# Nine up pairs by seven products, two low parts by accumulating DMA, and half-height score tiles in a two-layer hybrid attention block on Trainium2

## The chip, the core and the metric

The kernel runs on one core of one Trainium2 chip. Its metric is the time of one execution in device microseconds (us), the median of several runs; a profiled execution beside them leaves a trace. The engines are called by the profile's names: PE (TensorE, matmuls), PEld (its weight loads), DVE (VectorE), ACT (ScalarE), POOL (GpSimd) and SP (SyncE, which issues most DMAs). A line number such as L579 is a line of the kernel before.

## The reference, cut to what matters

512 tokens of 1024 features go through two layers, all in float32. Layer 0 has differential attention over all earlier tokens, layer 1 windowed attention with sinks; behind each stands a gated feed-forward block of 2816 hidden features.

```python
def swiglu(h, w_gate_up, w_down):
    g, u = jnp.split(h @ w_gate_up, 2, axis=-1)
    return (jax.nn.silu(g) * u) @ w_down
...
    for l in range(DEPTH):
        h = rms_norm(x, attn_norm[l])
        if l < N_A:
            x = x + diff_attention(h, cos, sin, da_w_qkv[l], ...)
        else:
            if l == N_A:
                kw, vw = shared_kv(x, cos, sin, kv_norm, w_kv, k_norm)
            x = x + swa_sink_attention(h, cos, sin, sw_w_q[j], ..., kw, vw)
        x = x + swiglu(rms_norm(x, ffn_norm[l]), w_gate_up[l], w_down[l])
```

In both attentions the scores are products over a head of 64 features. In layer 0 a pair of score matrices (two half heads) belongs to each head; in layer 1 four query heads share one key head, and a block of 128 queries sees its own block of keys and the one before.

## The kernel before, in words

**Split numbers.** A float32 matrix is multiplied as a sum of three products: each operand is split into a high part `hi` (a cast on ACT, L578, L267, L774) and a low part `lo` (source minus high part, a subtraction on DVE, L579, L268, L775), and PE adds hi·hi, hi·lo and lo·hi in PSUM (`mm3`, L288, and the loops at L704 and L790).

**Order.** PE's instructions are in the order in which the program writes them. The other engines' order is set by the scheduler from priorities; `tc.high_priority(offset=...)` moves a few instructions ahead (constants `BOOST`, `EVAC`, `NPRI`, `HOT`, `SW_BOOST`, `SW_EVAC`). SP issues weight loads in its own order and waits there for a free buffer.

**Attention stages.** Layer 0 works on four pairs of heads. For each, a list (`DA_STEPS`, `DA_STEPS3`) gives slots to the steps T (turn queries and keys, `flip`), C (scores, `score`), U (turn the softmax, `turn`), W (weigh values, `weigh`), N and B (norm); between slots `Fill.pull` writes matmuls of the next pair's projections into PE's order (`DA_FILL` us for a slot unit). `score` (L1009) multiplies half heads of 64 features: two matmuls of 64 rows each, one on the upper and one on the lower half of the array, into two banks. Layer 1 has 16 units of work (4 key heads by 4 query blocks); `SW_AT` holds six slots for each: turn the queries (`turn_q`), two scores, two turns of the softmax, weigh. There `q_evac` (L422) builds a tile whose columns hold a head's high part on 64 rows and its low part on the other 64, with a copy of the keys on both halves, so that a full-height matmul gives hi·hi and lo·hi at once; a score for one head is two matmuls (L1331, L1332), and one call of `score` does two heads.

**Feed-forward block.** The hidden features are cut into 11 pairs `q` of 256 gate and 256 up columns, worked in chunks (0, 1), (2, 3, 4), (5, 6, 7), (8, 9, 10): first the up products of each pair of the chunk, then the down products of the chunk. A plain pair (`up`, L627) takes 96 matmuls of 512 columns. A pair in `FAST` (`up7`, L662) uses a scheme of seven products of half blocks in place of eight: 14 products (seven for gate, seven for up) of 12 matmuls with 256 columns, with sums of weight blocks on DVE (L671, L672, L687, L689) and sums of results (L722 to L739). The down part (`down`, L753) uses the scheme for all pairs: seven factors `s`, each with a right side (weights `g`, `make_right`, four sums for each pair) and a left side (`make_left`), 6 matmuls of 512 columns for each factor and pair. `tokens` (L591) makes the summed token blocks once for a layer.

**Preparation ahead.** `Flow` (L463) writes the splits ahead of their use: `AHEAD` says how many uses ahead, rings of `HLB` = 8 buffers (hi, lo) and `AHB` buffers (left parts) bound it. Weight tiles `r` (up) and `g` (down) have three buffers each.

Of the kernel before, what the change touches and what calls it, by code (L numbers as in the profile page):

```python
# [17 lines left out]
P = 128  # L18
# [11 lines left out]
FAST = (2, 3, 5, 6, 8, 9)  # L30
AHEAD = {'w': 4, 'a': 4}
AHB = 5
WRAW = 3
XDB = 0
BOOST = 42
HOT = 1220
EVAC = 17
# [6 lines left out]
NPRI = 759  # L44
DA_FILL = 0.65


def DA_STEPS(T, C, U, W, N, B):
    return [
        (0, T, 0),  # L50
        (5, C, 0, 0),
        (5.4, T, 1),
        (5.78, C, 0, 1),
        (7.16, C, 1, 0),
        (11, C, 1, 1),
        (11.9, T, 2),
        (13.5, U, 0, 1),
        (17.5, U, 0, 0),
        (17.8, C, 2, 0),
        (19, T, 3),  # L60
        (20.59, U, 1, 0),
        (20.84, C, 2, 1),
        (22.01, W, 0, 0),
        (23.1, U, 1, 1),
        (24.5, C, 3, 0),
        (28.5, W, 0, 1),
        (30.5, N, 0),
        (31.9, C, 3, 1),
# [7 lines left out]
        (47.84, N, 1),  # L76
        (58.9, B, 1),
# [37 lines left out]
SW_K = [4, 5, 6, 12]  # L115
SW_AT = [5.2, 7.3, 8.7, 15.1, 16, 17.8, 8.8, 10.9, 12.3, 18.7, 19.6, 21.3, 10.1, 13.3, 14.8, 21.1, 22, 23.7, 14.7, 16.8, 18.3, 24.6, 25.5, 27.73, 16.7, 19.5, 20.9, 27.3, 28.2, 29.9, 21.66, 23.76, 25.16, 31.56, 32.46, 34.96, 26.5, 28.6, 30, 36.4, 37.3, 39, 31.1, 33.2, 34.6, 41, 41.9, 43.6, 37.3, 39.4, 40.8, 45.7, 48.1, 49.8, 39, 41.1, 42.5, 48.24, 49.8, 51.5, 43.1, 45.2, 46.6, 53.13, 53.9, 55.6, 45.6, 47.7, 49.1, 56.3, 56.83, 58.1, 49.9, 52, 53.4, 60.6, 61.36, 61.69, 52.53, 55.4, 56.8, 64, 64.1, 65.09, 57.5, 59.6, 61, 67.86, 68.3, 70.39, 61.5, 63.6, 65, 72.2, 72.3, 74.39]
SW_R = [-0.4, 13.7, 14.24, 39.07, 43.47, 47.06]
SW_F = 37.2
# [18 lines left out]
def tile_yoco_hybrid(  # L137
# [284 lines left out]
    def q_evac(ap, pt):  # L422
        q = ap.tile([P, 512], F32R, name=nm("q"), tag="q", bufs=QB)
        src = pt[:, 0:256].rearrange("p (s q) -> p s q", q=P)
        dst = q.rearrange("p (s j q) -> p s j q", j=2, q=P)
        a, b = slice(0, HD), slice(HD, P)
        with tc.high_priority(offset=pri["evac"]):
            for j, (own, other) in enumerate(((a, b), (b, a))):
                nc.scalar.copy(dst[own, :, j], src[own])
                nc.vector.tensor_tensor(dst[other, :, j], src[own], dst[own, :, j].bitcast(F32), op=ALU.subtract)  # L430
        return q

# [66 lines left out]
    class Ffn:  # L499
# [69 lines left out]
        def load_r(self, q, j):  # L569
            if q < NQ:  # L570
                r = self.rs[q, j] = self.fp.tile([P, 2, 4, 256], F32, name=nm("r"), tag="r", bufs=WRAW)
                for c in range(2):
                    nc.sync.dma_start(out=r[:, c], in_=self.wu[:, 4 * j:4 * j + 4, c * FFN + q * 256:c * FFN + (q + 1) * 256])

        def split(self, src, shape):
            hi = wp.tile(shape, F32R, name=nm("hi"), tag="hi", bufs=HLB)
            lo = wp.tile(shape, F32R, name=nm("lo"), tag="lo", bufs=HLB)
            nc.scalar.copy(hi, src)  # L578
            nc.vector.tensor_tensor(lo, src, hi.bitcast(F32), op=ALU.subtract)  # L579
# [920 lines left out]
```

## Time and profile before

| | us |
|---|---|
| median of three runs | 1151.5 (1151.07 to 1151.97) |
| the profiled execution | 1150.19 |
| its span in the trace | 1148.1 |
| layer 0 attention, 47 to 268 us of the span | 221.0 |
| layer 0 feed-forward, chunks 2 to 4, 341.9 to 615.3 | 273.4 |
| layer 1 attention, 615.3 to 791 | 175.7 |

Times in a profile line are us from the span's start, or durations; "mean ns" is one instruction's. In the timeline a line gives start, duration, engine, line, operation, out<-in, tile sizes and a count, with the engine's idle time ahead of it in brackets. A matmul's duration includes its way through the array, so matmuls that follow each other overlap in the records: the step from one start to the next is the price. The same holds for DVE. In the table of waits a line is: engine, line, and what it waited for, the sum in us, how often, the longest.

### The profile page before, as it was taken

The numbers are of one execution on the slowest core, as the hardware profiler recorded it, in microseconds if no ns is written. First come the engines' busy times: TensorE is split into PE (matmuls) and PEld (weight loads), VectorE is DVE, ScalarE is ACT, GpSimd is POOL, SyncE is SP. The second block draws the span as 40 slices with busy tenths as digits, with TensorE's granted clock in tenths as the row PEclk, the third lists the DMA queues.
The fourth block names the chain that finished last, engine by engine and source line by source line (L and its number), as shares of the span: only waits on it lengthen the run. The fifth ranks groups of instructions, "written<-read, shape, count | busy, mean of one in ns | idle before, by whom it ended". The sixth has DMA issues, their size and how long they took to land.

```text
span 1148.1 us, 18912 instructions
## 1 busy us (share of the span) xinstructions
PE 1123.8 (98%) x6806; PEld 979.7 (85%) x6806; DVE 995.2 (87%) x2368; ACT 659.4 (57%) x1463; POOL 20.4 (2%) x32
## 2 busy tenths in 40 slices
PE   8999999999999999999999999989999999999998
PEld 7878888778889889989988888777989989988986
DVE  5979798979999998898888797988899898898877
ACT  6565756554556455455446579787545545545533
POOL 0100000000000000000300000000000000000000
PEclk9999999999999999999999999999999999999999
DMA  6312122122723323405202221020634405314201
GB/s 194 111 56 69 47 70 65 47 74 79 252 72 114 109 71 124 137 18 167 76 1 82 84 74 56 20 74 11 206 115 147 144 4 171 98 63 148 74 1 74
DMA packets 86591, 103.29 MB, mean 90 GB/s; under 512 B 5161, under 2 KB 68034, under 8 KB 86498
## 3 DMA queue, kind: packets, MB, share of 16 engines
q1 hardware_dynamic: 86064, 100.97, 27.3%
q0 software_dynamic: 384, 1.11, 0.4%
q8 instruction: 53, 0.87, 0.3%
q14 instruction: 40, 0.33, 0.1%
q10 hardware_dynamic: 50, 0.01, 0.0%
HBM read 99.98 MB, written 2.10 MB: 89 GB/s over the span
## 4 chain that ended last, share of the span: by engine, by line
PE 76%; DVE 16%; ACT 4%; DMA 2%; issue 1%; SPq 0%; DVEq 0%; ACTq 0%
PE acc L706 12%; PE acc L289 10%; PE acc L291 10%; PE acc L290 10%; PE tr L791 9%; PE acc L791 8%; PE tr L706 7%; DVE lo L268 2%; PE po L706 1%; DVE s L1024 1%; DVE hss L382 1%; PE po L791 1%; PE po L290 1%; PE tr L1020 1%; DVE xs L460 1%
## 5 line engine op out<-in xcount | busy, mean ns | idle before, releaser
L578 ACT CAST hi<-g 128x512 fp32r<-128x512 f32 x154 | 95.2, 618 | 113.1 <-PE acc L290 104.4
L578 ACT CAST hi<-r 128x512 fp32r<-128x512 f32 x160 | 98.6, 620 | 75.5 <-PE acc L706 44.2
L289 PE MATMUL acc<-hi,hTh 128*128 128x256 f32 (+1 forms) x384 | 137.6, 358 | 2.7 <-ACT hTh L866 0.9
L291 PE MATMUL acc<-hTh,lo 128*128 128x512 f32 (+1 forms) x384 | 136.4, 355 | 0.7 <-DVE lo L579 0.5
L289 PE MATMUL acc<-hTh,hi 128*128 128x512 f32 (+1 forms) x384 | 136.2, 355 | 0.0
L290 PE MATMUL acc<-hTl,hi 128*128 128x512 f32 (+1 forms) x384 | 136.1, 354 | 0.0
L291 PE MATMUL acc<-hi,hTl 128*128 128x256 f32 (+1 forms) x384 | 130.1, 339 | 0.3 <-DVE hTl L296 0.2
L290 PE MATMUL acc<-lo,hTh 128*128 128x256 f32 (+1 forms) x384 | 129.7, 338 | 0.4 <-DVE lo L268 0.4
L579 DVE TENSOR_TENSOR lo<-r,hi 128x512 fp32r<-128x512 f32 x160 | 106.2, 690 | 18.4 <-ACT hi L578 18.0
L579 DVE TENSOR_TENSOR lo<-g,hi 128x512 fp32r<-128x512 f32 x154 | 105.5, 691 | 12.6 <-ACT hi L578 12.2
L774 ACT CAST ah<-lf 128x256 fp32r<-128x256 f32 x154 | 60.5, 404 | 81.2 <-PE acc L791 32.2
L289 PEld LDWEIGHTS acc<-hi,hTh 128*128 128x128 f32 x384 | 72.9, 190 | 13.5 <-issue 3.7
L291 PEld LDWEIGHTS acc<-hTh,lo 128*128 128x128 f32 x384 | 72.5, 189 | 12.0 <-DVE lo L579 1.3
L267 ACT CAST hi<-raw 128x512 fp32r<-128x512 f32 x96 | 57.4, 618 | 43.8 <-PE acc L291 26.8
L290 PEld LDWEIGHTS acc<-hTl,hi 128*128 128x128 f32 x384 | 72.6, 189 | 10.1 <-DVE hTl L296 0.2
L706 PE MATMUL acc<-th,hi 128*128 128x256 f32 x288 | 81.1, 282 | 0.0
L706 PE MATMUL acc<-tl,hi 128*128 128x256 f32 x288 | 81.1, 282 | 0.0
L706 PE MATMUL acc<-th,lo 128*128 128x256 f32 x288 | 81.0, 281 | 0.0
L289 PEld LDWEIGHTS acc<-hTh,hi 128*128 128x128 f32 x384 | 72.6, 189 | 9.7
L291 PEld LDWEIGHTS acc<-hi,hTl 128*128 128x128 f32 x384 | 72.7, 189 | 9.3 <-DVE hTl L867 0.7
L290 PEld LDWEIGHTS acc<-lo,hTh 128*128 128x128 f32 x384 | 73.1, 190 | 5.7 <-DVE lo L268 0.7
L268 DVE TENSOR_TENSOR lo<-raw,hi 128x512 fp32r<-128x512 f32 x96 | 64.6, 687 | 10.0 <-ACT hi L267 9.9
(278 smaller groups left out, 3181.5 us busy)
## 6 DMA issues: line engine op xcount, KB each, us to landing
r<-in_w_gate_up_dram SPq DMA_DIRECT2D x80, 512.0 KB, 5.1
g<-in_w_down_dram SPq DMA_DIRECT2D x88, 256.0 KB, 5.1
raw<-in_da_w_qkv_dram SPq DMA_DIRECT2D x30, 256.0 KB, 3.1
raw<-in_da_w_qkv_dram SPq DMA_DIRECT2D x8, 512.0 KB, 3.6
raw<-in_da_w_o_dram SPq DMA_DIRECT2D x8, 512.0 KB, 3.5
raw<-in_w_gate_up_dram SPq DMA_DIRECT2D x8, 512.0 KB, 4.3
raw<-in_sw_w_q_dram SPq DMA_DIRECT2D x8, 512.0 KB, 3.4
raw<-in_sw_w_o_dram SPq DMA_DIRECT2D x8, 512.0 KB, 3.4
```

Source lines behind the costliest of these rows:

```text
L267: nc.scalar.copy(hi, part)
L268: nc.vector.tensor_tensor(lo, part, hi.bitcast(F32), op=ALU.subtract)
L289: nc.tensor.matmul(dst, sh, mh, start=start, stop=False)
L290: nc.tensor.matmul(dst, sh, ml, start=False, stop=False)
L291: nc.tensor.matmul(dst, sl, mh, start=False, stop=stop)
L382: nc.vector.tensor_reduce(out=ss[:, t, :], in_=sq.rearrange("p (g e) -> p g e", e=HD), axis=AX.X, op=ALU.add)
L460: nc.vector.tensor_tensor(xsl, xsl, pt, op=ALU.add)
L578: nc.scalar.copy(hi, src)
L579: nc.vector.tensor_tensor(lo, src, hi.bitcast(F32), op=ALU.subtract)
L706: nc.tensor.matmul(dst, l[:, k, :], r[:, k, :], start=fresh and k == 0 and i == 0, stop=k == 3 and i == 2, skip_group_check=not fresh)
L774: nc.scalar.copy(ah, src)
L791: nc.tensor.matmul(bank, l[:, tk], r, start=fresh and i == 0 and n == 0, stop=i == len(qs) - 1 and n == 2, skip_group_check=not fresh)
```

## The change

It has these parts:

- `FAST` goes from six pairs to nine (2 to 10), so that pairs 4, 7 and 10 of both layers go through `up7`. The token blocks 5 and 6 swap places; `tokens` is written as a generator that is run through at once.
- `DLO = (1, 5)`: for the right factors 1 and 5 of all 11 pairs of both layers (44 times), the low part is no longer subtracted on DVE. ACT writes the negated cast into `lo`, and GpSimd issues a DMA that adds the source to it in place. The sums of right blocks are made in another order, so that the source of such a DMA isn't overwritten; their number stays four a pair.
- `LATE = 2`: in a chunk's down part, factors 0 and 1 of all pairs but the last come first, then factors 0 and 1 of the last pair, then the rest.
- `AHEAD` is 6 and 5 (from 4 and 4), `AHB` 6 (from 5).
- Scores: layer 1 uses 64-row matmuls as layer 0 did (`half_rows`, six matmuls for two heads, all four heads of a unit in one call), so queries are split into a plain high and low tile (two instructions in place of four). In layer 0 the scores of the first two query tiles (up to 256 keys) of both heads share a pair of banks and are one step.
- Slots and priority constants have new values (a line or two of the tables stands in the diff), and some tiles are allocated earlier in their pools.

```diff
-FAST = (2, 3, 5, 6, 8, 9)
-AHEAD = {'w': 4, 'a': 4}
-AHB = 5
+FAST = (2, 3, 4, 5, 6, 7, 8, 9, 10)
+AHEAD = {'w': 6, 'a': 5}
+AHB = 6
...
+DLO = (1, 5)
+LATE = 2
+GS = 5
+NTH = 4
+FIRST = lambda nc: nc.sync
-BOOST = 42
+BOOST = 24
-EVAC = 17
+EVAC = 6
...
-NPRI = 759
-DA_FILL = 0.65
+NPRI = 184
+DA_FILL = 0.6368
...
-        (5, C, 0, 0),
-        (5.4, T, 1),
-        (5.78, C, 0, 1),
+        (6.4, C, 0, (0, 1)),
+        (6.69, T, 1),
...
     def q_evac(ap, pt):
-        q = ap.tile([P, 512], F32R, name=nm("q"), tag="q", bufs=QB)
...
+        q = [ap.tile([P, 256], F32R, name=nm("q"), tag=f"q{z}", bufs=QB) for z in "hl"]
+        split_evac(*q, pt[:, 0:256])
         return q
+
+    def half_rows(banks, cols, q, k):
+
+        for a, b in ((0, 0), (0, 1), (1, 0)):
+            for c in range(2):
+                rows = slice(c * HD, (c + 1) * HD)
+                nc.tensor.matmul(banks[c][:, cols], q[a][rows], k[b][rows], start=a + b == 0, stop=a == 1)
...
+        def split(self, src, shape, move=False):
             hi = wp.tile(shape, F32R, name=nm("hi"), tag="hi", bufs=HLB)
             lo = wp.tile(shape, F32R, name=nm("lo"), tag="lo", bufs=HLB)
+            if move:
+                nc.scalar.activation(lo, src, AF.Copy, scale=-1.0)
+                nc.gpsimd.dma_start(out=lo.bitcast(F32), in_=src, accum_op=ALU.add)
             nc.scalar.copy(hi, src)
-            nc.vector.tensor_tensor(lo, src, hi.bitcast(F32), op=ALU.subtract)
+            if not move:
+                nc.vector.tensor_tensor(lo, src, hi.bitcast(F32), op=ALU.subtract)
             return hi, lo
...
-                    rights[s, q] = [z[:, 0, :] for z in self.split(g[:, (0, 1, 4, 0, 2, 3, 1)[s]:][:, 0:1, :], [P, 1, 512])]
-                    if s == 0:
-                        tt(g[:, 0, :], g[:, 2, :], g[:, 0, :], op=ALU.subtract)
-                        tt(g[:, 4, :], g[:, 3, :], g[:, 0, :], op=ALU.subtract)
+                    two = GS - 1 if GS == 6 else 0
+                    if s == 2:
+                        tt(g[:, two, :], g[:, 3, :], g[:, 4, :], op=ALU.subtract)
+                    src = (0, 1, two, 4, 2, 3, two)[s]
+                    rights[s, q] = [z[:, 0, :] for z in self.split(g[:, src:src + 1, :], [P, 1, 512], s in DLO)]
+                    if s == 1:
+                        tt(g[:, 4, :], g[:, 2, :], g[:, 0, :], op=ALU.subtract)
                         tt(g[:, 2, :], g[:, 3, :], g[:, 2, :], op=ALU.subtract)
-                    if s == 1:
-                        tt(g[:, 1, :], g[:, 1, :], g[:, 4, :], op=ALU.subtract)
+                    if s == 2:
+                        tt(g[:, two, :], g[:, 1, :], g[:, two, :], op=ALU.subtract)
...
-                uses = [(flow.prep("w", make_right(s, q)), flow.prep("a", make_left(s, q), self.ready[q])) for q in qs]
+                todo.append((s, b, fresh, post))
+            heads, n = LATE, len(qs) - 1
...
+            order = [(z, i) for z in todo[:heads] for i in range(n)] + [(z, n) for z in todo[:heads]] +                 [(z, i) for z in todo[heads:] for i in range(n + 1)]
+            for (s, b, fresh, post), i in order:
+                q = qs[i]
+                uses = flow.prep("w", make_right(s, q)), flow.prep("a", make_left(s, q), self.ready[q])
                 for t in range(2):
-                    for i in range(len(qs)):
-                        flow.step(part(s, b, t, i, fresh, post), *uses[i])
+                    flow.step(part(s, b, t, i, fresh, post), *uses)
...
-        def score(self, i, h):
+        def score(self, i, hs):
...
+            cols = [slice(x * 256, x * 256 + n) for x in range(len(hs))]
+            for x, h in enumerate(hs):
+                half_rows(pts, cols[x], [z[:, h, tk] for z in self.qkT], [z[:, 2 + h, 0:n] for z in self.qkT])
...
-        def score(u, pr):
+        def score(u):
...
-                nc.tensor.matmul(pt[:, cs], q[:, gsl], kT[0][:, kv, ks], start=True, stop=False)
-                nc.tensor.matmul(pt[:, cs], q[:, gsl], kT[1][:, kv, ks], start=False, stop=True)
...
+            for s in range(2):
+                half_rows(pts, cols[s], [z[:, s * P:(s + 1) * P] for z in qs[u]], [z[:, kv, ks] for z in kT])
```

Two places show how the instructions move. The first is PE in layer 1, at the scores of the first unit that sees two key blocks (`tr` is a PSUM bank, `kTs` the keys, `q` the queries, `acc` the banks of the projection that fills in between). Before, its second pair of heads stood alone, behind projection matmuls and a turn of another unit:

```order
L419 MATMUL tr_8059<-ident,td_7735 128x128 x2
L1331 MATMUL tr_8067<-kTs_7256,q_7927 128x256
L1332 MATMUL tr_8067<-kTs_7257,q_7927 128x256
L1331 MATMUL tr_8067<-kTs_7256,q_7927 128x256
L1332 MATMUL tr_8067<-kTs_7257,q_7927 128x256
L289 MATMUL acc_7983<-hi_7946,hTh_7198 128x512
L290 MATMUL acc_7983<-lo_7947,hTh_7198 128x512
```

Now, on PE at the same unit, all four heads stand in one block (`q_8235` the high part, `q_8236` the low part):

```order
L433 MATMUL tr_8400<-kTs_7623,q_8235 128x256
L433 MATMUL tr_8401<-kTs_7623,q_8235 128x256
L433 MATMUL tr_8400<-kTs_7624,q_8235 128x256
L433 MATMUL tr_8401<-kTs_7624,q_8235 128x256
L433 MATMUL tr_8400<-kTs_7623,q_8236 128x256
L433 MATMUL tr_8401<-kTs_7623,q_8236 128x256
L433 MATMUL tr_8400<-kTs_7623,q_8235 128x256
L433 MATMUL tr_8401<-kTs_7623,q_8235 128x256
L433 MATMUL tr_8400<-kTs_7624,q_8235 128x256
L433 MATMUL tr_8401<-kTs_7624,q_8235 128x256
L433 MATMUL tr_8400<-kTs_7623,q_8236 128x256
L433 MATMUL tr_8401<-kTs_7623,q_8236 128x256
```

Two blocks of four full-height matmuls, apart, became one block of twelve half-height ones that alternate between two banks.

The second place is the down part of chunk (2, 3, 4) in layer 0, at factor 5 (`g` are right blocks, one tile for each pair; `lf` left blocks, `al` their low parts). Before, DVE made the low parts of factor 5 (`lo_5061`, `lo_5088`, `lo_5099`) between left parts and additions to `xs`:

```order
L775 TENSOR_TENSOR al_5046<-lf_4480,ah_5045 128x256
L579 TENSOR_TENSOR lo_5061<-g_4360,hi_5060 128x512
L803 TENSOR_TENSOR xs<-xs,acc_5049 128x512
L579 TENSOR_TENSOR lo_5088<-g_4635,hi_5087 128x512
L775 TENSOR_TENSOR al_5073<-lf_4810,ah_5072 128x256
L775 TENSOR_TENSOR al_5080<-lf_4205,ah_5079 128x256
L803 TENSOR_TENSOR xs<-xs,acc_5068 128x512
L775 TENSOR_TENSOR al_5092<-lf_4480,ah_5091 128x256
L579 TENSOR_TENSOR lo_5099<-g_4793,hi_5098 128x512
```

Now they stand on ACT, as negated casts (`ACTIVATE`) behind the third high part of the factor (`hi_5197`), and each is followed by a DMA on GpSimd; DVE goes from the low parts of factor 4 to those of factor 6:

```order
L583 CAST hi_5165<-g_4324 128x512
L790 CAST ah_5170<-lf_4762 128x256
L583 CAST hi_5182<-g_4599 128x512
L790 CAST ah_5187<-lf_4204 128x256
L583 CAST hi_5197<-g_4882 128x512
L581 ACTIVATE lo_5166<-g_4324 128x512
L581 ACTIVATE lo_5183<-g_4599 128x512
L581 ACTIVATE lo_5198<-g_4882 128x512
L790 CAST ah_5202<-lf_4479 128x256
```

Three subtractions left DVE's queue there, and three casts and three DMAs came onto ACT's and GpSimd's.

More of the change, by code (lines that the diff above doesn't have):

```diff
@@ L593, in tokens @@
             fp, (hh, hl) = self.fp, self.hT
-            self.th, self.tl = (fp.tile([P, 4, 4, 256], F32R, name=nm(z), tag=z) for z in ("th", "tl"))
-            ra, rb = (fp.tile([P, 10, 256], F32, name=nm("g"), tag="g", bufs=3) for _ in range(2))
+            ra, rb = (fp.tile([P, 2 * GS, 256], F32, name=nm("g"), tag="g", bufs=3) for _ in range(2))
             b11, b12, b21, b22 = ra[:, 0:4], ra[:, 4:8], rb[:, 0:4], rb[:, 4:8]
@@ L624, in block @@
                 return [z[:, k:k + 4, t:t + 256] for z in self.hT]
+            if n - 3 == NTH:
+                return [z[:, 0:4, 256:512] for z in self.hT]
             return self.th[:, n - 3], self.tl[:, n - 3]
@@ L632, in go @@
                 def go():
-                    parts[m, c, j] = self.split(self.rs[q, j][:, c, :, m * P:(m + 1) * P], [P, 4, P])
+                    parts[m, c, j] = self.split(self.rs[q, j][:, c, :, m * P:(m + 1) * P], [P, 4, P], (m, c, j) in DLO)
                     if m and c:
@@ L681, in go @@
                 def go():
-                    parts[f, c] = self.split(source(f, c), [P, 4, P])
+                    parts[f, c] = self.split(source(f, c), [P, 4, P], (f, c) in DLO)
                     r0, r1 = self.rs[q, 0], self.rs[q, 1]
@@ L843, in rest @@
                         (self.up7 if q in FAST else self.up)(flow, q)
+                        if q == 1 and NTH == 3:
+                            flow.step(lambda: self.later())
                 end = qs is chunks[-1]
@@ L1016, in score @@
             tk = slice(i * P, (i + 1) * P)
-            for a, b in ((0, 0), (0, 1), (1, 0)):
+            cols = [slice(x * 256, x * 256 + n) for x in range(len(hs))]
+            for x, h in enumerate(hs):
+                half_rows(pts, cols[x], [z[:, h, tk] for z in self.qkT], [z[:, 2 + h, 0:n] for z in self.qkT])
+            for x, h in enumerate(hs):
                 for c in range(2):
-                    rows = slice(c * HD, (c + 1) * HD)
-                    nc.tensor.matmul(pts[c][:, 0:n], self.qkT[a][rows, h, tk], self.qkT[b][rows, 2 + h, 0:n],
-                                     start=a + b == 0, stop=a == 1)
-            for c in range(2):
-                with tc.high_priority(offset=pri["evac"]):
-                    nc.vector.tensor_tensor_reduce(
-                        out=self.sb[i][h][:, c, 0:n], in0=pts[c][:, 0:n], in1=maskD[:, 512 - n:512], scale=1.0,
-                        scalar=-3e38, op0=ALU.add, op1=ALU.max, accum_out=self.mx[:, 2 * h + c:2 * h + c + 1])
-            if h == 1:
+                    with tc.high_priority(offset=pri["evac"]):
+                        nc.vector.tensor_tensor_reduce(
+                            out=self.sb[i][h][:, c, 0:n], in0=pts[c][:, cols[x]], in1=maskD[:, 512 - n:512], scale=1.0,
+                            scalar=-3e38, op0=ALU.add, op1=ALU.max, accum_out=self.mx[:, 2 * h + c:2 * h + c + 1])
+            if hs[-1] == 1:
                 self.soften(i)
```

158 lines of the change are left out of this document (76 added, 82 removed).

## Prediction

> **What bounds the kernel now.** I read the page's head first, then a table of busy time by stretch (cut where the chain of waits changes its lines), then the waits inside the feed-forward stretch. All times are of the profiled execution.
>
> ```profile
> span 1148.1 us, 18912 instructions
> PE 1123.8 (98%) x6806; PEld 979.7 (85%) x6806; DVE 995.2 (87%) x2368; ACT 659.4 (57%) x1463; POOL 20.4 (2%) x32
> ```
>
> The columns below are: stretch, its length, then busy time and count of PE, PEld, DVE, ACT, POOL, granted clock, DMA share, GB/s.
>
> ```profile
> 47.00:268.00 221.00, 215.32 (x1327) 176.37 (x1328) 188.38 (x652) 127.26 (x308) 1.55 (x3) 1.00 0.19 60
> 361.91:381.93 20.02, 20.02 (x169) 20.02 (x169) 17.60 (x35) 11.95 (x25) 0.00 (x0) 1.00 0.34 106
> 381.93:403.75 21.82, 21.82 (x98) 18.03 (x97) 18.70 (x31) 7.11 (x14) 0.00 (x0) 1.00 0.31 97
> 403.75:433.02 29.27, 29.27 (x128) 23.74 (x128) 28.65 (x55) 16.81 (x37) 0.00 (x0) 1.00 0.30 103
> 433.02:524.16 91.14, 91.14 (x561) 81.81 (x560) 80.58 (x145) 47.70 (x98) 0.00 (x0) 1.00 0.32 105
> 341.89:433.02 91.13, 91.13 (x561) 81.81 (x560) 83.55 (x149) 47.75 (x99) 0.00 (x0) 1.00 0.35 112
> 615.30:791.00 175.70, 166.38 (x1005) 143.39 (x1004) 145.14 (x492) 139.95 (x375) 1.13 (x2) 0.99 0.19 63
> ```
>
> The feed-forward chunk of three pairs (341.89 to 433.02) is full of matmuls without a gap: a pair of seven products takes 20.02 us, the plain pair 21.82, the down part 29.27. Only the attention stretches leave TensorE idle: 221.00 - 215.32 = 5.7 us in the first, 175.70 - 166.38 = 9.3 in the second. So the feed-forward part gets faster only by fewer matmul microseconds, and only as long as VectorE (88 to 92% busy there) keeps up. TensorE's waits between 294 and 615 us are two, of 0.5 us together:
>
> ```profile
> PE tr L791 <- DVE al L775: 0.3, 1, 0.3
> PE acc L291 <- DVE lo L579: 0.2, 1, 0.2
> ```
>
> **The change part by part.**
>
> *Three more pairs by seven products in each layer.* Pairs 4, 7 and 10 go from 96 matmuls of 512 columns to 168 of 256. The rows price both: 21.82 against 20.02 us, 1.80 saved, six times: **-10.8 us**, all on the path, if VectorE and ScalarE keep up.
>
> *VectorE in the feed-forward part.* Its real price per instruction is the step from start to start in a full queue (first a line of the groups with its mean of 690 ns, then the timeline: start, duration, line):
>
> ```profile
> L579 DVE TENSOR_TENSOR lo<-r,hi 128x512 fp32r<-128x512 f32 x160 | 106.2, 690 | 18.4 <-ACT hi L578 18.0
> ...
> 363.51 0.43 DVE L557 TENSOR_TENSOR lf<-lf 128x256 f32<-128x256 f32 x1
> 363.85 0.42 DVE L558 TENSOR_TENSOR lf<-lf 128x256 f32<-128x256 f32 x1
> 364.18 0.42 DVE L559 TENSOR_TENSOR lf<-lf 128x256 f32<-128x256 f32 x1
> 364.52 1.23 DVE L689 TENSOR_TENSOR raw<-r,raw 128x1024 f32<-128x1024 f32 x1
> 365.65 2.50 DVE L579 TENSOR_TENSOR lo<-r,hi 128x512 fp32r<-128x512 f32 x4
> ```
>
> That is 0.335 us for 256 columns, 1.13 for 1024, and (2.50 - 0.69)/3 = 0.60 for 512. A seven-product pair has 14 low parts (8.4), 4 sums of 1024 (4.5), one multiply of 512 (0.6) and 12 operations of 256 (4.0): 17.5 us under 20.02 of TensorE. A plain pair has 8 low parts, 2 multiplies, 4 sums of 256: 7.3. The down part of three pairs has 21 low parts of right factors, 12 sums, 14 additions to xs (47 x 0.60 = 28.2) and 21 left low parts (7.0): 35.2. So a chunk held 2 x 17.5 + 7.3 + 35.2 = 77.5 us, where the rows above show 80.6 and 83.6 busy. It will hold 3 x 17.5 + 35.2, less the six low parts that go to the DMA (3.6): **84.1 us beside 3 x 20.02 + 29.27 = 89.3 of TensorE**. Scaled as the two chunks above exceed their count (80.58/77.5 = 1.04, 83.55/77.5 = 1.08) this is 87.5 to 90.8. Part of that excess is only the longer record of an instruction with a gap behind it (0.69 against 0.60), so I take the lower end and stalls of 0.2 us a chunk: **+1.2 us** for six chunks, with 0 and 1.5 a chunk (9) as bounds. Preparing six uses ahead in place of four evens out the two halves of a chunk.
>
> *Low parts by accumulating DMA.* ScalarE writes the negated cast, GpSimd issues the DMA that adds the source. ScalarE gets 44 casts, and six more for each new pair, at the price of the first row below, under a busy time of 48 of 91 us: nothing. What matters is the landing. Before has no accumulating DMA; the nearest rows are GpSimd's own loads of the same size, and the weights beside them (the cast's group; GpSimd's timeline; the table of DMA issues with KB and us to landing; the stretch in which the DMA is fullest):
>
> ```profile
> L578 ACT CAST hi<-g 128x512 fp32r<-128x512 f32 x154 | 95.2, 618 | 113.1 <-PE acc L290 104.4 <-issue 7.2 <-PE tr L791 1.4
> 192.80 0.72 POOL L509 DMA_DIRECT2D gb<-in_ffn_norm_dram  x1 [157.68 <-DVE u L398]
> gb<-in_ffn_norm_dram POOLq DMA_DIRECT2D x4, 256.0 KB, 3.5
> g<-in_w_down_dram SPq DMA_DIRECT2D x88, 256.0 KB, 5.1
> ...
> 386.00:390.00 4.00, 4.00 (x20) 3.30 (x19) 3.97 (x6) 1.12 (x2) 0.00 (x0) 1.00 0.97 322
> ```
>
> How much time it has follows from the ring of eight buffers. One use of a right factor is six matmuls, 29.27/21 = 1.39 us (0.23 a matmul). On ScalarE the three negated casts of factor 5 stand behind the cast of its third high part, which waits for the buffer of six uses before the first need: five uses, 7.0 us, remain. Less 0.62 for the cast, **6.3 us from issue to landing**. An accumulating DMA reads its target as well as its source, so the bounds are 3.5 (as the load) and 10.2 (twice the weight load); I take 4.5, nearest to GpSimd's own row, and no cost. Factor 1 has more room, since its buffers come free under the products. The new waits: behind GpSimd's DMA, which waits for the cast, only further such DMAs are queued; behind the matmul, which waits for the landing, stands all of TensorE; and SP's load of the next chunk's right factors waits until the DMA has read the tile, with up weights queued behind it, which are needed a pair later.
>
> *Scores in 64-row tiles.* The first attention already does this, the second does not (start, duration; window at 55 us, then at 698):
>
> ```profile
> 55.23 0.40 PE L291 MATMUL acc<-hi,hTl 128*128 128x512 f32 x1
> 55.56 0.39 PE L1020 MATMUL tr<-qkT 64*128 64x256 f32 x2
> 55.78 0.40 PE L1020 MATMUL tr<-qkT,qkT 64*128 64x256 f32 x4
> 56.11 0.50 PE L289 MATMUL acc<-hi,hTh 128*128 128x512 f32 x1
> ...
> 698.30 0.28 PE L1331 MATMUL tr<-kTs,q 128*128 128x256 f32 x1
> ...
> 698.77 0.40 PE L289 MATMUL acc<-hi,hTh 128*128 128x512 f32 x1
> ```
>
> Four full-height matmuls of 256 columns take 0.47 us, 0.119 each. A block of six half-height ones lies between 55.23 + 0.23 (the step of a 512-column matmul) and 56.11: 0.65 us, where three pairs run side by side would be 0.36. So the halves do run in pairs, and going into and out of that mode costs 0.29 us a block. In the second attention a unit goes from 8 x 0.119 = 0.95 to 6 x 0.119 + 0.29 = 1.00 us for 12 units, and from 0.48 to 0.65 for the 4 units with one key block (128 columns, taken as half of 0.119): **+1.3 us**. In the first attention two blocks become one for the first two of four query tiles in four pairs: 8 x 0.29 = **-2.3 us**.
>
> A rule speaks against the 64-row tiles: the Trainium skill, TensorEngine Tiling (Array Packing), section Tiling Modes (Key Properties), says that changing the tiling mode drains the engine; its Overview gives up to 2x for a contraction of at most 64. By that speedup alone the second attention would gain 12 x 0.24 + 4 x 0.12 = 3.3 us instead of losing 1.3. The 0.29 us row sides with the drain, and the sum goes by the row.
>
> *Waits in the second attention.*
>
> ```profile
> PE tr L1331 <- DVE q L430: 4.6, 6, 1.7
> PE tr L1331 <- DVE mx L1337: 0.9, 1, 0.9
> L430 DVE TENSOR_TENSOR q<-tr,q 64x256 fp32r<-64x256 f32 x32 | 13.5, 422 | 5.3 <-ACT q L429 4.4
> ```
>
> Half of the 9.3 us idle waits for the query's split, two ScalarE casts and two VectorE subtractions in turn. Now it is one of each, 16 VectorE operations fewer (5.4 us), and the score is placed 3.2 to 4.4 slots behind the query's turn where it was 2.1. What is late next is the softmax (exponent and scaling on ScalarE, 80% busy there), which starts only when all four heads are scored. I take **-3.0 us** of the 4.6, with 0 and -9.3 as bounds. For the re-placed steps of the first attention I take **-0.5** (0 to -3).
>
> *Nothing for the rest.* The reordered start of the down part (third pair's first two factors last) only moves matmuls; it gives the third pair's loads and left factors two more uses, and nothing waited there. The seven-factor sums are as many as before. Token sums, pool placement and the constants of priority move work on engines that TensorE did not wait for at those places. If that cover fails, it shows as waits of the kind priced above.
>
> **Sum.** -10.8 + 1.2 + 1.3 - 2.3 - 3.0 - 0.5 = -14.1 us on a span of 1148.1. The profiled execution took 1150.19 us, 2.1 more than its span, and the median of the three runs is 1151.5; I carry the difference over: **1137.4 us**.
>
> **The rivals.**
>
> *A, the accumulating DMA lands late (slower).* Place: the third matmul of factor 5, later of factor 1. It decides from 6.3 us on; each microsecond beyond costs one in each of eight chunks, and the gain is used up at 6.3 + 14.1/8 = 8.1 us. At 10.2 us it costs 8 x 3.9 = 31 us, and about 8 more at factor 1: 1151.5 - 14.1 + 39 = **1176 us**. For it: the target is read too, and weight loads fill the DMA (97% in 386 to 390 us) just when the next pair begins. Against it: 3.5 us in GpSimd's own row. A variant (0.02 of its chance) is that a busy VectorE keeps GpSimd from issuing; at 564 us neither blocked the other (VectorE's timeline, then GpSimd's):
>
> ```profile
> 564.41 0.41 DVE L739 TENSOR_TENSOR lf<-lf,acc 128x256 f32<-128x256 f32 x1
> 564.74 0.42 DVE L558 TENSOR_TENSOR lf<-lf 128x256 f32<-128x256 f32 x1
> ```
>
> ```profile
> 564.51 0.55 POOL L1250 DMA_DIRECT2D gsw<-in_sw_q_norm_dram  x1 [327.72 <-DVE lf L557]
> ```
>
> The Trainium skill, SBUF — State Buffer, section SBUF: two separate sides, describes that variant: descriptors are not written while VectorE holds the shared port in a two-port mode, 0.62 us becoming 3.1. By its 2.5 us the landing would be 7.0 and the cost 0.7 x 8 = 6 us; the issue of 0.55 us beside back-to-back VectorE work here does not agree. Chance of A: 0.10.
>
> *B, VectorE becomes the bound of the feed-forward part.* It decides when its 84.1 us a chunk grow by more than 6%. At the upper scale of 90.8 us a chunk it costs 1.5 us in six chunks, 9 in place of 1.2: **1145 us**. For it: one of two chunks measured 8%. Against: TensorE waited 0.5 us though VectorE was 98% busy through the down part. Chance 0.17.
>
> *C, the second attention gains nothing or loses*, because its new steps wait for the softmax: 3.0 + up to 5 us back, **1140 to 1145 us**. Chance 0.13. That the halves do not run in pairs is excluded by the 0.65 us row.
>
> **How the numbers follow.** The forecast case has 0.60. Its range runs from all 9.3 us of idle time gone and no stalls (1137.4 - 6.3 - 1.2 = 1130) to 1142; B and C reach to 1147. The range is 1130 to 1147, which leaves out most of A and some of the low side. A measurement of this kernel can tell 0.2% (2.3 us) from no change; only A, and the worst of B with C, come near that, so faster 0.87, same 0.04, slower 0.09.
>
> **What would show it.** Right: pairs 4, 7, 10 at 20.0 us without a gap; VectorE at 93 to 98% in a chunk of 89.3 to 89.6 us; accumulating DMAs landing under 6 us; half-height blocks of 12 at 1.0 us; fewer query waits. Wrong: waits of TensorE on the DMA at factor 5 (A), on low parts all through the seven-product pairs (B), or more than 9 us of idle time in the second attention (C).

## The result, and the profile after

The changed kernel took **1130.99 us** (median of 4 runs, 1130.75 to 1132.55) beside 1151.28 before: ratio 0.9826 (0.9813 to 0.9838), 20.3 us (1.7%) faster. The forecast was 1137.4 (1130 to 1147). The direction held, and the time lies at the low end of the range; the gain is 6 us larger than the sum. How far the mechanism held is told below, and in one step it did not. The profiled execution took 1132.55 us with a span of 1130.8, 17.3 below the span of before.

The page's head of the changed kernel, then its table of busy time by stretch (columns as in the prediction). The stretches are those of before, cut near the same places of the work (the second attention's ends differ by 0.7 and 1.4 us, all of it matmul time, so its idle time can be compared and its length cannot): first attention, start of the feed-forward part, its three chunks, the chunk (2, 3, 4) and its parts, second attention.

```profile
span 1130.8 us, 20321 instructions
PE 1110.2 (98%) x7302; PEld 986.4 (87%) x7302; DVE 1010.1 (89%) x2410; ACT 710.9 (63%) x1569; POOL 55.1 (5%) x76
```

```profile
47.00:266.30 219.30, 214.19 (x1332) 176.78 (x1333) 187.94 (x652) 127.55 (x309) 1.60 (x3) 0.99 0.20 61
266.30:341.06 74.76, 73.14 (x420) 63.33 (x419) 70.34 (x129) 40.46 (x75) 3.59 (x4) 1.00 0.55 164
341.06:609.86 268.80, 268.80 (x1900) 252.04 (x1899) 255.51 (x467) 170.94 (x354) 16.97 (x21) 1.00 0.39 109
341.06:430.42 89.36, 89.36 (x633) 83.82 (x632) 86.25 (x156) 56.81 (x117) 5.26 (x6) 1.00 0.44 122
381.12:401.14 20.02, 20.02 (x169) 20.02 (x169) 18.78 (x36) 13.62 (x29) 2.44 (x3) 1.00 0.50 132
401.14:430.42 29.28, 29.28 (x129) 23.74 (x128) 28.83 (x56) 19.29 (x40) 2.83 (x4) 1.00 0.48 123
609.86:779.00 169.14, 164.72 (x1074) 138.41 (x1073) 136.60 (x476) 132.82 (x358) 7.46 (x14) 1.00 0.20 62
```

The chunk is 89.36 us where it was 91.13, with TensorE busy in all of it: pair 4 takes 20.02 us, its down part 29.28. VectorE is 97% busy (86.25 of 89.36) and holds nobody up. In the second attention TensorE's idle time fell from 9.3 us to 4.4 (169.14 - 164.72).

Markers in the program place the 17.3 us: 0.8 up to pair 2 of layer 0, 5.3 from there to the end of that feed-forward part (its last matmul, 616.03 us before and 609.86 after; the 615.3 of the table before lies 0.7 us ahead of it), 6.0 in the second attention and the start of the next feed-forward part, 5.1 in the rest. The two feed-forward terms are the six pairs (6 x 1.80 = 10.8). The second attention gained 6.0 where the sum had 3.0 less 1.3, 1.7. Three of the longest waits of TensorE after (of the others the longest, 1.8 us, is at the start of the kernel):

```profile
PE acc L290 <- DVE vl L1011: 2.1, 1, 2.1
PE acc L290 <- ACT hTh L296: 1.5, 1, 1.5
PE tr L1391 <- DVE mx L1361: 1.1, 1, 1.1
```

None is on the query: the row of 4.6 us in six places is gone. None is on a DMA. The accumulating transfers in the table of DMA issues (KB each, median us to landing):

```profile
lo<-g POOLq DMA_DIRECT2D x44, 256.0 KB, 3.6
```

GpSimd's issues of factor 5 in the chunk of pairs 2, 3, 4:

```profile
416.64 2.67 POOL L582 DMA_DIRECT2D lo<-g  x3 [15.35 <-PE acc L807]
```

TensorE's first matmul with that low part:

```profile
422.13 0.40 PE L807 MATMUL acc<-lo,ah 128*128 128x512 f32 x1
```

From the first issue to the first need there are 422.13 - 416.64 = 5.5 us (the ring argument gave 6.3), and the landing takes 3.6 in the median, 3.2 at least and 8.7 at most. Four of the 44, at factor 1 of the chunk (0, 1) in both layers (issued at 306.12, 311.08, 824.75 and 829.71), took 6.5 to 8.7 us, more than the 6 that the prediction named as the sign of being right; the DMA was 92 to 95% busy there. TensorE did not wait for them, since factor 1 has more room, as the prediction said. A score block of the second attention (start, duration) runs from 673.52 + 0.23 to 674.74, 0.99 us where 1.00 was forecast:

```profile
673.52 0.39 PE L292 MATMUL acc<-hi,hTl 128*128 128x512 f32 x1
673.84 0.98 PE L433 MATMUL tr<-kTs,q 64*128 64x256 f32 x12
674.74 0.44 PE L420 MATMUL tr<-ident,td 128*128 128x128 f32 x2
```

### The profile page after: what moved, and what is told of

It is laid out like the page before. It is cut to its first block, busy times and chain, and to the rows that moved or that the text cites. A ratio compares the mean times of both kernels' runs of the same rounds, so it can differ in the third digit from the quotient of the medians.

```text
span 1130.8 us, 20321 instructions
## 1 busy us (share of the span) xinstructions
PE 1110.2 (98%) x7302; PEld 986.4 (87%) x7302; DVE 1010.1 (89%) x2410; ACT 710.9 (63%) x1569; POOL 55.1 (5%) x76
## 4 chain that ended last, share of the span: by engine, by line
PE 79%; DVE 11%; ACT 5%; DMA 3%; issue 1%; SPq 0%; DVEq 0%; ACTq 0%
PE acc L719 18%; PE tr L719 11%; PE tr L807 9%; PE acc L807 8%; PE acc L290 7%; PE acc L292 7%; PE acc L291 7%; PE po L719 2%; PE tr L433 2%; DVE lo L269 1%; PE po L291 1%; ACT s L1372 1%; PE tr L420 1%; PE po L292 1%; PE po L807 1%
## 5 line engine op out<-in xcount | busy, mean ns | idle before, releaser
L719 PE MATMUL acc<-th,hi 128*128 128x256 f32 x432 | 121.7, 282 | 0.0
L719 PE MATMUL acc<-tl,hi 128*128 128x256 f32 x432 | 121.6, 282 | 0.0
L719 PE MATMUL acc<-th,lo 128*128 128x256 f32 x432 | 121.6, 281 | 0.0
L583 ACT CAST hi<-raw 128x512 fp32r<-128x512 f32 x108 | 67.0, 620 | 63.3 <-PE tr L719 18.7
L719 PEld LDWEIGHTS acc<-th,hi 128*128 128x128 f32 x432 | 81.5, 189 | 0.0
L719 PEld LDWEIGHTS acc<-tl,hi 128*128 128x128 f32 x432 | 81.4, 188 | 0.0
L719 PEld LDWEIGHTS acc<-th,lo 128*128 128x128 f32 x432 | 81.3, 188 | 0.0
L268 ACT CAST hi<-raw 128x512 fp32r<-128x512 f32 x96 | 57.6, 620 | 34.7 <-PE acc L292 23.9
L585 DVE TENSOR_TENSOR lo<-g,hi 128x512 fp32r<-128x512 f32 x110 | 75.2, 684 | 1.0 <-ACT hi L583 0.9
L269 DVE TENSOR_TENSOR lo<-raw,hi 128x512 fp32r<-128x512 f32 x96 | 64.5, 685 | 10.5 <-ACT hi L268 10.0
L582 POOL DMA_DIRECT2D lo<-g x44 | 38.6, 977 | 723.6 <-DMA g<-in_w_down_dram 179.4
L585 DVE TENSOR_TENSOR lo<-raw,hi 128x512 fp32r<-128x512 f32 x108 | 72.6, 684 | 0.3
```

The source lines that it names most:

```text
L268: nc.scalar.copy(hi, part)
L269: nc.vector.tensor_tensor(lo, part, hi.bitcast(F32), op=ALU.subtract)
L582: nc.gpsimd.dma_start(out=lo.bitcast(F32), in_=src, accum_op=ALU.add)
L719: nc.tensor.matmul(dst, l[:, k, :], r[:, k, :], start=fresh and k == 0 and i == 0, stop=k == 3 and i == 2, skip_group_check=not fresh)
```

## The experiments

The theory was that the feed-forward part gains the matmul time of six pairs as long as the sum of VectorE's work fits a chunk, and that the second attention gains by waits removed. Times are medians; ratios are to the kernel before; "the changed kernel" stands at 1131.0.

**Nine pairs alone.** The kernel before with

```
-FAST = (2, 3, 5, 6, 8, 9)
+FAST = (2, 3, 4, 5, 6, 7, 8, 9, 10)
```

> The kernel before with one edit: pairs 4, 7 and 10 also by seven products. No accumulating DMA, no other order, no more preparation ahead. The saving of matmul time is 10.8 us, 1151.3 to 1140.5 if VectorE keeps up; with stalls of 0.5 to 1.5 us in six chunks 1143 to 1149.

1182.0, ratio 1.0262 (1.0246 to 1.0278): 31 us slower than before. Neither case foresaw that. By the two profiled executions (1179.8 against 1148.1) TensorE is idle 28.9 us more, and its busy time grew by 2.8 where 10.8 less was due, with half-clock windows behind the waits: 28.9 + 13.6 - 10.8 = 31.7. TensorE's longest waits in it (total, places, longest):

```profile
PE tr L791 <- DVE al L775: 20.9, 7, 5.4
PE acc L791 <- DVE al L775: 6.8, 2, 3.4
```

VectorE's timeline (start, duration) at the start of the down part of pairs 2, 3, 4, whose matmuls begin at 402.32:

```profile
403.56 0.41 DVE L739 TENSOR_TENSOR lf<-lf,acc 128x256 f32<-128x256 f32 x1
403.89 0.68 DVE L762 TENSOR_TENSOR g<-g 128x512 f32<-128x512 f32 x1
404.49 0.68 DVE L766 TENSOR_TENSOR g<-g 128x512 f32<-128x512 f32 x1
405.10 0.68 DVE L763 TENSOR_TENSOR g<-g 128x512 f32<-128x512 f32 x1
405.70 0.68 DVE L764 TENSOR_TENSOR g<-g 128x512 f32<-128x512 f32 x1
406.30 0.41 DVE L556 TENSOR_TENSOR lf<-lf 128x256 f32<-128x256 f32 x1
...
408.85 1.08 DVE L775 TENSOR_TENSOR al<-lf,ah 128x256 fp32r<-128x256 f32 x3
```

TensorE at the third use of the down part (idle time before it in brackets):

```profile
409.31 0.79 PE L791 MATMUL tr<-hi,al 128*128 128x512 f32 x1 [4.97 <-DVE al L775]
```

The long wait (3.4 to 5.4 us) is at one place in each chunk of three pairs: the third use of the down part, the last pair's first left factor. Its low part (L775) stands in VectorE's queue behind five sums of right blocks (L762 to L766, 0.60 us each, one of them in the lines left out) that nobody needs yet, and behind sums of left blocks. In the six-pair kernel the last pair was plain and left VectorE free there (18.70 of 21.82 us).

So two new theories. **T1**: the order of the sums decides. The change moved them from behind factor 0 to behind factors 1 and 2, an edit that the prediction had put at nothing. **T2**: the accumulating DMAs or the late third pair, either of them, keep the wait away. Four runs cross these edits in the changed kernel.

**No accumulating DMA.** `DLO = (1, 5)` became `DLO = ()`.

> The changed kernel with all low parts on VectorE, none by accumulating DMA. VectorE gets six low parts of 0.60 us more in each chunk of three pairs: the 85.6 to 86.3 us measured become 89.2 to 89.9, beside 89.36 of TensorE. Theory (VectorE's own count decides): stalls of 0.5 to 1 us a chunk, 1134 to 1137. Rival B's stronger form (the DMA lows carry the gain): 1.5 us and more a chunk, 1140 or above. If VectorE has hidden room (part of its busy time is only the longer record of an instruction with a gap behind it): within 1 us of 1131.

1134.6, ratio 0.9852 (0.9838 to 0.9865): 3.6 us, inside the theory's range. The trace does not show its mechanism, a stall in each chunk: TensorE waits `acc` for `al` 2.7 us in four places, two of them in the chunk (0, 1), and the second chunk of three pairs has no gap.

**Old order and preparation.** `AHEAD` to 4 and 4, `AHB` to 5, `LATE` to 0.

> The changed kernel with weights prepared four uses ahead in place of six, left factors four in place of five, and the down part's old order (all three pairs' factors in turn). The prediction put no cost on the order and let preparation ahead even out VectorE's load. If evening out is not needed (VectorE's 86 us of a 89.36 us chunk lie evenly enough): within 1 us of 1131. If it is: stalls of up to 1.5 us in each of six chunks, 1134 to 1140. The room of the accumulating transfer falls from six uses to four, 5.6 less 0.6 us for the cast is 5.0, still above the 3.6 it takes, so rival A would not show.

1131.8, ratio 0.9830 (0.9817 to 0.9845): within 1 us. With the DMAs in place neither the late third pair nor the longer preparation is needed.

**Neither.** Both edits together; the new order of the sums stays.

> The changed kernel without the accumulating DMAs, with the down part's old order and weights and left factors four uses ahead; the new order of the factor sums stays (two sums behind factor 1 and two around factor 2, where before all three of a tile stood behind factor 0). With the old order of the sums as well (the kernel before with nine pairs) TensorE waited 3.4 to 5.4 us at the third pair's first left factor in each chunk. VectorE's work that stands ahead of that left factor's low part, by the text of the code: 9.6 us there, 7.2 in the changed kernel, which uses it 2.8 us later, so 4.4; here 5.4. Theory T1 (the order of the sums decides): 1133 to 1138. Theory T2 (accumulating DMAs or the late third pair, either of them, is what keeps the wait away): 1160 or above.

1131.2, ratio 0.9824 (0.9808 to 0.9839), no different from the changed kernel and below T1's own range (1133 to 1138). Its first chunk of three pairs, in the table by stretch:

```profile
339.19:428.54 89.35, 89.35 (x631) 83.82 (x630) 87.19 (x160) 51.49 (x108) 0.00 (x0) 1.00 0.33 100
```

VectorE's timeline at the start of its down part, at 399.27:

```profile
400.41 0.41 DVE L752 TENSOR_TENSOR lf<-lf,acc 128x256 f32<-128x256 f32 x1
400.74 0.41 DVE L560 TENSOR_TENSOR lf<-lf 128x256 f32<-128x256 f32 x1
401.07 0.41 DVE L561 TENSOR_TENSOR lf<-lf 128x256 f32<-128x256 f32 x1
401.41 0.68 DVE L585 TENSOR_TENSOR lo<-g,hi 128x512 fp32r<-128x512 f32 x1
402.01 0.42 DVE L791 TENSOR_TENSOR al<-lf,ah 128x256 fp32r<-128x256 f32 x1
402.35 0.68 DVE L782 TENSOR_TENSOR g<-g 128x512 f32<-128x512 f32 x1
```

The left parts follow the last product at once, and the sums (L782, L775) come after the low part that TensorE waits for: 2.7 us into the down part where it was 6.5 (408.85 - 402.32). VectorE carries all the low parts, 87.2 of 89.35 us, without a stall. T2 falls: with the new sums both the accumulating DMAs and the new order of the down part can be left out. So does the theory that VectorE's count decides. The late order and the longer preparation without the DMAs (the run at 1134.6) are worse than neither.

**The old sums.** No accumulating DMAs, and in `make_right`

```
-if s == 1: g4 = g2 - g0;  g2 = g3 - g2
-if s == 2: g0 = g3 - g4 (ahead of the split);  g0 = g1 - g0
+if s == 0: g0 = g2 - g0;  g4 = g3 - g0;  g2 = g3 - g2
+if s == 1: g1 = g1 - g4
```

> The changed kernel without the accumulating DMAs and with the old order of the factor sums (three behind factor 0, one behind factor 1); the third pair's late start and the longer preparation ahead stay. By the same count 11.4 us of VectorE's work stand ahead of the third pair's left factor, 2.8 later in use: 8.6, near the 9.6 of the kernel before with nine pairs. T1: 2 to 4 us of wait in each of six chunks and half-clock stretches behind them, 1150 to 1170. T2: within 3 us of the run without the accumulating DMAs, 1134 to 1138.

1153.7, ratio 1.0012 (1.0001 to 1.0024), 19.1 us above the run that differs only by the sums (1134.6). T1 stands. TensorE's longest wait in it:

```profile
PE tr L805 <- DVE al L789: 13.1, 10, 2.9
```

The down parts of its first two chunks of three pairs, 34.33 and 33.93 us in place of 29.28:

```profile
397.88:432.21 34.33, 31.37 (x128) 24.71 (x127) 32.96 (x63) 16.34 (x35) 0.00 (x0) 0.95 0.15 45
492.29:526.22 33.93, 31.21 (x129) 24.41 (x128) 33.01 (x63) 16.37 (x35) 0.00 (x0) 0.95 0.15 47
```

The first down part lost 5.0 us, of which 3.0 are idle time of TensorE. The other 2.1 are in its busy time, 1.7 of it one window of half clock (0.95 in the row is the mean). That showed in several runs and is taken up below. The longest wait is 2.9 us here and 5.4 in the kernel before with nine pairs, whose sums are the same; the late order, the longer preparation and the new attentions lie between the two, and no run separates them. The old sums beside the accumulating DMAs were not run; there a sum overwrites the source of such a DMA.

**A late transfer.** The source added a second time to factor 5 of each chunk's last pair:

```
+for _ in range(move):
     nc.gpsimd.dma_start(out=lo, in_=src, accum_op=ALU.add)
...
-self.split(src, shape, s in DLO)
+self.split(src, shape, (s in DLO) + (s == 5 and q == qs[-1]))
```

> The changed kernel, in which the source is added twice, by two accumulating DMAs in turn, to the low part of the down part's sixth factor (number 5) of each chunk's last pair; the low part's values are wrong by that. In the changed kernel's trace the third DMA is issued about 418.4 us and lands 3.6 us later, its matmul stands at 424.9. The second add is issued after the landing and lands about 426: 0.9 to 1.3 us late in each of eight chunks. Theory (rival A is real, with its threshold near 6.3 us from issue): 1138 to 1142, with TensorE waiting for a DMA at that factor. If the transfer has more room than the ring argument gives it: 1131.

1181.2, ratio 1.0258 (1.0238 to 1.0277). Rival A's mechanism is real, and the run is dearer than I priced it, 50 us and not 7 to 11. GpSimd issues the second add in the chunk of pairs 2, 3, 4:

```profile
425.60 0.88 POOL L583 DMA_DIRECT2D lo<-g  x1 [4.19 <-DMA lo<-g]
```

SP's queue had begun with the weights of the next pairs:

```profile
422.09 0.34 SPq L568 DMA_DIRECT2D g<-in_w_down_dram  x1
```

TensorE's matmul that needs the low part:

```profile
433.99 0.79 PE L808 MATMUL acc<-lo,ah 128*128 128x512 f32 x1 [6.81 <-DMA lo<-g]
```

That wait over the whole run, and then the busy times around the first one, in windows of 3.41 us:

```profile
PE acc L808 <- DMA lo<-g: 35.9, 8, 6.8
```

```profile
426.73:430.14 3.41, 0.44 (x2) 0.01 (x1) 0.78 (x2) 0.62 (x1) 0.00 (x0) 1.00 0.87 231
430.14:433.55 3.41, 0.00 (x0) 0.00 (x0) 0.00 (x0) 0.00 (x0) 0.00 (x0) 0.50 0.90 249
433.55:436.96 3.41, 2.98 (x7) 2.40 (x8) 1.13 (x2) 0.38 (x1) 0.00 (x0) 0.50 0.44 154
```

The second add took 8.4 us (425.60 to 433.99), while the next pairs' weights were loading (since 422.09) and the DMA was 87 to 90% busy. In the last chunk of each layer, behind which SP loads no weights, it took 3.3 us (620.58 to 623.90 and 1164.01 to 1167.29), and the waits there are the two shortest (1.25 and 1.45 us). The first adds are issued before those loads are let go. So the landing time depends on where the issue falls. Behind the wait the clock stood at 0.50. By the two profiled executions (1176.8 against 1130.8) 34.5 of the 46.0 us are idle time of TensorE and 11.5 its longer busy time: 1.3 us for each of the 35.9 waited.

**The wait filled.** The same kernel with 18 spare matmuls ahead of the one that waits:

```
+spare = att("po") if last else acc()
+for _ in range(18):
+    nc.tensor.matmul(spare, ah[:, tk], hi, start=True, stop=True)
```

> The kernel in which the source is added twice to the low part of factor 5 of each chunk's last pair (1181.2), with 18 matmuls of 512 columns (4.2 us) into a spare bank between the last pair's first matmul and the one that waits. There TensorE waited 35.9 us in eight places, 4.5 each, and the granted clock fell to 0.50 behind seven of them, for 3.4 or 6.8 us at a time. Theory (an idle stretch of TensorE takes the clock down, and that costs beyond the wait): the spare matmuls fill the wait, the clock stays at 1.00, and 8 to 12 us come back: 1168 to 1173, though as much matmul work is added as the wait was long. If the clock falls for another reason, or the spare matmuls simply add to the time: 1180 or above.

1183.3, ratio 1.0288 (1.0259 to 1.0317). The forecast of time fell. The clock did as expected: of seven low stretches in the chunks (eleven windows of 3.4 us) two windows are left. But the waits in eight places are of different length, 1 to 7 us, the spare matmuls are 4.36 us in each (35 us), and 10.6 us of waits remain. The run also has a wait of its own, 4.5 us in three places for additions to `xs`. More was added than the clock gave back. What the low clock costs is not measured by this run.

**Pair 1 as well.** `FAST` from 1 to 10.

> The changed kernel with pair 1 by seven products as well. Matmul time falls by 1.8 us a layer, 3.6 in all: 1127.4 if the token sums are ready and VectorE keeps up. But between 266 and 341 us VectorE is busy 70.3 of 74.8 us, and the pair adds 10 us to it, 80 beside 73: if VectorE is the bound there, 5 to 7 us a layer are lost, 1137 to 1145.

1150.6, ratio 0.9996 (0.9986 to 1.0007): 19.6 us lost, where the upper case was 14 (1145). TensorE waits for VectorE and ScalarE in pair 1 and at the down part behind it (7.2 us for `al`, 3.5 for `lo`), and the clock in its two stretches (295.41 to 349.38 us) is 0.82 and 0.87. VectorE is the bound there, as expected, and the clock about doubled the price: by the profiled executions TensorE is idle 13.0 us more than in the changed kernel, and its busy time is 7.4 longer where 3.6 less was due.

**The second attention.** It gained 6.0 us by the trace where the sum had 1.7. First, all of it as before, in the changed kernel:

> The changed kernel with the whole second attention as before: the old split, full-height scores in two halves a unit, the old places. The old split with the new places stands at 1143.8, the new split with the old places at 1143.3. By the trace the second attention gained 6 us, 1.7 of it one stretch of half clock: 1137 to 1138. If a feed-forward part that starts at another time matters too, it lies outside 1135 to 1140. The forecast's own terms (3.0 of waits, less 1.3 for the tiles) would have 1132.7.

1139.5, ratio 0.9898 (0.9881 to 0.9914): the second attention is worth **8.5 us**, more than the 6.0 of the markers and above the 1137 to 1138 expected. Busy times in this kernel from 616 to 800 us:

```profile
616.00:800.00 184.00, 173.38 (x1045) 149.47 (x1044) 152.78 (x509) 142.13 (x378) 1.15 (x2) 0.99 0.18 60
```

The changed kernel:

```profile
616.00:800.00 184.00, 179.91 (x1174) 151.75 (x1173) 153.16 (x517) 139.45 (x370) 1.32 (x3) 1.00 0.23 69
```

Idle time is 10.6 against 4.1 us, 6.5 of the gain. One window of half clock (1.7 us) is in the old one and none in the new. Together 8.2.

Then the old split and full-height matmuls at the new places (`q_evac` and the eight matmuls of a unit as before, `SW_AT` new):

> The changed kernel, but in the second attention the query is split by the old two casts and two subtractions and scored by eight full-height matmuls a unit; the new table of places stays. Span of the changed kernel 1130.8 us, median 1131.0; before 1151.3. The second attention gained 6.0 us by the trace, where the sum had 1.7. Theory S (the wider distance from the query's turn to its score took the waits away; the shorter split and the 64-row tiles give nothing): 1130.4 to 1131.5, with the row of TensorE waiting for the query absent. Theory Q (the shorter split took them away): about 4.6 us of that wait come back, 1135 to 1137.

1143.8, ratio 0.9927 (0.9912 to 0.9942). And the new split at the old places (`SW_AT`, `SW_K`, `SW_R`, `SW_F` of before):

> The changed kernel with its new split and 64-row scores, but every step of the second attention at its old place (the score at the place of the old first half, 2.1 slots behind the query's turn). Theory S (distance): the query wait and most of the gain go, 1135 to 1137. Theory Q (shorter split): at most 1 us is lost, 1131 to 1132. If both are needed, each of this run and the one with the old scores lies 2 to 4 us above 1131.

1143.3, ratio 0.9930 (0.9916 to 0.9943). Theory S (the wider distance alone took the waits away) and theory Q (the shorter split alone) both fall: each half of the change alone is about 4 us **worse** than neither (1139.5). TensorE's longest waits in the second attention of the first of the two runs:

```profile
PE po L290 <- ACT ph L296: 3.5, 3, 2.7
PE po L291 <- DVE pl L297: 3.4, 5, 2.0
```

And of the second:

```profile
PE tr L1391 <- DVE pl L297: 5.4, 2, 4.7
```

With the old split at the new places the weighing waits for the softmax's split; with the new split at the old places the next turn of the softmax waits. Of the query wait (4.6) 2.1 us are left in the first and 0.3 in the second, so on that row alone theory Q was nearly right. Not all of the loss is waits. Beside the run with neither, by the profiled executions, the first (in the slowest of its six executions) has 3.7 us more idle time and 3.6 more busy time, the second 1.1 us less idle time and 4.5 more busy time, with five half-clock windows while TensorE had work where the run with neither has one. A table of places is tuned to the operations that it places.

**The first attention as before.** Its steps, its priorities and its unmerged scores (`(5, C, 0, (0,))`, `(5.78, C, 0, (1,))` and so on):

> The changed kernel with the first attention's scores unmerged, its steps at their old places and its old priorities. By the prediction's terms (2.3 for merged blocks, 0.5 for the steps) 2.8 us come back: 1133.8. The trace's marker at the end of the first attention moved by 2.1 to 2.4 us, and the start of the feed-forward part gave 1.3 of it back: if that loss stands whatever the first attention does, 1133.2; if the start of the feed-forward part waits for something else anyway, 1131.5 to 1132.

1134.4, ratio 0.9851 (0.9838 to 0.9864): 3.4 us, by 2.8 forecast. TensorE's busy time is 1111.0 us at full clock, where the changed kernel's is 1110.2 with one window of half clock, 1108.5 without: 2.5 us, the term of 2.3 for eight blocks.

## Why the prediction was right, and where it was not

- *Six pairs, -10.8*: held. 5.3 and 5.1 us in the two feed-forward parts, pairs of 20.02 us without a gap.
- *VectorE, +1.2 of stalls from its total in a chunk*: the stalls were 0, and the total was the wrong thing to price. Counted at 87.7 us without the DMAs, it was 87.2 busy and stalled nobody. What stalls TensorE is what stands in VectorE's queue ahead of one low part.
- *"Nothing for the rest", the sums "as many as before"*: **this step failed**. I priced the number of the sums and not their place. The place is worth 19.1 us (1153.7 against 1134.6), and nine pairs with nothing else of the change lose 31 us to before. That the forecast came out is in this part luck: the change held that edit, and I had not seen what it does. It is also where rival B's mechanism was: a bound by VectorE at one instruction, not over the chunk.
- *Accumulating DMAs, 0*: held, 3.6 us in 5.5 of room. They were put in the sum as what keeps VectorE under TensorE; the run with neither says that they are not needed (1131.2). Rival A's price of 1 us for each microsecond waited was somewhat low (1.3), and its bound of 10.2 us for a landing was not reached in the changed kernel (8.7 at most); the doubled transfer cost 50 us because it landed later than I expected.
- *64-row tiles in the second attention, +1.3*: 0.99 us a block held for the 12 units with two key blocks. For the four with one, a unit takes 0.91 us where it took 0.78 (I had 0.65 and 0.48: four matmuls of 128 columns took 0.39 us before, 666.29 to 666.68, and not half of 0.47). By these steps the tiles cost 12 x 0.05 + 4 x 0.13 = 1.1 us. Busy time shows less: without half-clock windows it is 1108.5 after, and 1110.1 less 1.7 (one window), 1108.4, with the old second attention.
- *Merged blocks, -2.3, and the first attention's steps, -0.5*: 2.5 in busy time, 3.4 in all.
- *Waits in the second attention, -3.0 of 9.3*: right in kind, mis-sized. All 4.6 of the query wait went and 1.9 of others, 6.5 together between 616 and 800 us, and with them a half-clock window of 1.7. I had taken part of one row and not asked what the row does to the clock. I also misread the table of places: the score now stands 3.2 to 6.0 slots behind the query's turn (not 3.2 to 4.4), where it was 2.1 to 3.2.

The six pairs (10.4 by the trace; no run undoes them alone) and the two attentions, each undone in the changed kernel, sum to 10.4 + 8.5 + 3.4 = 22.3 us; the whole gave 20.3. The rest of 2.0 is not settled; one half-clock window (below) is about of that size.

## What to carry to other kernels

Where an engine is nearly as busy as TensorE (VectorE at 97% here), a comparison of sums over a stretch is not enough: list what stands in its queue ahead of each result that TensorE needs next, and move work that nobody needs yet behind it. Placement tables and the operations they place are one edit, and half of it can be worse than none (by 4 us here). An idle stretch of TensorE should be priced with the clock that follows it.

## What the runs showed of the hardware

The granted clock falls to 0.50 for 3.41 us at a time, behind a window of that length in which TensorE was idle for a good part. Four places, cut in windows of 3.41 us (TensorE's busy time stands behind the length, the clock third from the end). The kernel before, in its second attention:

```profile
764.68:768.09 3.41, 1.99 (x13) 1.37 (x12) 3.36 (x20) 3.41 (x11) 0.00 (x0) 1.00 0.02 5
768.09:771.50 3.41, 3.41 (x11) 2.87 (x11) 3.21 (x8) 3.36 (x12) 0.00 (x0) 0.50 0.00 0
```

The changed kernel, in its first attention:

```profile
44.80:48.21 3.41, 1.35 (x10) 1.15 (x10) 2.19 (x6) 2.67 (x7) 0.00 (x0) 1.00 0.44 150
48.21:51.62 3.41, 3.41 (x11) 2.73 (x11) 2.24 (x6) 1.05 (x3) 0.00 (x0) 0.50 0.56 163
```

The changed kernel with the old second attention, and then the kernel before with nine pairs:

```profile
723.09:726.50 3.41, 2.17 (x10) 1.49 (x11) 3.35 (x11) 1.75 (x4) 0.00 (x0) 1.00 0.05 19
726.50:729.91 3.41, 3.41 (x13) 3.02 (x12) 2.43 (x13) 2.26 (x8) 0.00 (x0) 0.50 0.00 0
```

```profile
502.38:505.79 3.41, 0.00 (x0) 0.00 (x0) 3.41 (x8) 0.00 (x0) 0.00 (x0) 1.00 0.00 0
505.79:509.20 3.41, 2.83 (x7) 2.25 (x8) 3.41 (x8) 1.02 (x2) 0.00 (x0) 0.50 0.02 5
```

Idle time alone does not sort the windows. 1.42 us idle (3.41 - 1.99) and even 1.24 (3.41 - 2.17) took the next window to half clock. In the kernel before, 13.7 us ahead of the first of these rows, 1.68 us (3.41 - 1.73) did not; the clock of the window behind it is 1.00:

```profile
751.02:754.43 3.41, 1.73 (x12) 1.35 (x11) 3.21 (x12) 3.36 (x10) 0.00 (x0) 1.00 0.48 163
```

In the traces with such windows every one with over 1.9 us idle was followed by half clock, and of those with 1.2 to 1.8 some were and some were not; what decides there is open. A window lost costs 1.71 us (half of 3.41) if TensorE has work all through it. The changed kernel's profiled execution had one, with a mean clock of 0.998 and a span of 1130.8; the three others had 1.000, and spans of 1129.0 to 1129.4. The difference is of that size, so it is the likely reason why the profiled execution lies above the median, and the first attention's gain, 0.8 by the markers, is 2.5 without that window.

The Trainium skill, TensorE: Matmul & The Clock Gate, Part 1: The HAM clock gate, has the halved clock and a free-running window of 3413 ns. Both agree with these rows. It names an idle window, and idle gaps of over about 3.4 us, as what brings the clock down; here windows with as little as 1.2 us of idle time did, though not each of them, and the measurement decides.
